# Two-layer backbone with split fp32 products: second scale block loaded into raw-token places, first shift sum written to another place, sign of the sink logits taken later

## The chip, the cores and the metric

The kernel runs on one core of one Trainium2 chip. The metric is the time of one execution in device microseconds. Three executions of the kernel before took 1580.73, 1581.42 and 1584.02 us; the median, 1581.42 us, is the time before.

## What is computed

Two layers over 256 context tokens and 1024 latent tokens of 1024 channels. Each layer norms the tokens, scales and shifts them by numbers that a conditioning vector gives (`adaln`), mixes them (layer 0: attention in windows with sink logits; layer 1: latent attention) and adds the result behind a gate. What the change touches is the start of layer 0: `adaln`, the norm, and the product with `w_in`; and the sink logits, which join the softmax much later.

```python
def rms_norm(u, g):
    y = u * lax.rsqrt(jnp.mean(u * u, axis=-1, keepdims=True) + EPS)
    return y * g

def adaln(cond, w, bias):
    m = jax.nn.silu(cond) @ w + bias
    return jnp.split(m, 3, axis=-1)          # shift, scale, gate

def reference(x, c, ctx, c_ctx, ada_w, ada_b, norm_g, final_g, ...):
    for i in range(DEPTH):                   # DEPTH = 2
        shift_x, scale_x, gate_x = adaln(c, ada_w[i], ada_b[i])
        shift_c, scale_c, gate_c = adaln(c_ctx, ada_w[i], ada_b[i])
        hx = rms_norm(x, norm_g[i]) * (1.0 + scale_x[:, None]) + shift_x[:, None]
        hc = rms_norm(ctx, norm_g[i]) * (1.0 + scale_c) + shift_c
        if i == 0:                           # softmax over [scores, sink]
            yx, yc = window_gqa(hx, hc, a_w_in[0], a_sink[0], a_w_out[0], ...)
        else:
            yx, yc = latent_attention(hx, hc, b_w_in[0], ...)
        x = x + gate_x[:, None] * yx
        ctx = ctx + gate_c * yc              # not behind the last layer
    return rms_norm(x, final_g)
```

## The kernel before

**Numbers.** Every large product is made of fp32 operands that are split in a high and a low half; `mm3` (L128 to L130) makes one product of three matmuls: high by high, low by high, high by low. The high half of the normed tokens is written by ACT (L425), the low half by DVE (L426, which needs the high half). Weight pieces are split the same way: ACT casts the high half (L123), and L124 subtracts on POOL (now and then on DVE). So PE can only start a product when ACT and then DVE, or ACT and then POOL, are done.

**The opening.** The tokens come as ten tiles of 128 (two of context, then eight latent ones), which work in five pairs `p`. `ld_x(i)` loads a tile raw (L394, tile 0 to a place of a ring, tiles 1 to 9 to nine places of a tile `raw`); `sq_x(i)` squares it on ACT (L401), makes its norm in small operations of DVE and POOL (L402, L403) and writes the normed tile on DVE (L404) to the ring `xr`, four places at 34, 38, 42 and 48 of the arena. `T0(p, q)` turns two channel blocks of a pair by PE (L414, eight or four transposes into a PSUM bank), `H0` writes the high and low halves of the turned and scaled tokens (L425, L426), and `M0` multiplies them with the first block of `w_in` (`mm3`); its sums are copied to `Vraw` (L441, L443), one place for each pair.

**The scale and shift of layer 0.** There are two blocks of 512 scale columns and two of shift columns. The weights of the first scale block come in eight pieces (`ld_first`, L743) into the four places of the ring `astage`; `half` multiplies them with the conditioning vectors on PE (L186) and spreads the sums over partitions (`cols`, L205, then L213 and L216 on DVE). The second scale block (`ada0.fetch(3, astage)`, L179) follows in the same four places as soon as PE has read the first, is multiplied by `ada0.products` (L186) and read in `cols`. The shift blocks aren't multiplied on PE: DVE weighs them row block by row block (`weigh`, L193 for the first row block and L195 for the seven others, two conditioning vectors each), into the sums `acc0[0]` and `acc0[1]`, two places of 512 floats each. `acc0[0]` stands at 48 of the arena, where the last place of the ring `xr` is, `acc0[1]` at 42; both are read by `cols(0, ...)` (L205) only after the first projections of the next part. Layer 1's and the gate's blocks are weighed later in the same way.

**Small inputs.** `load_small` loads the unit matrix, two small tables and the sink logits on ACT's DMA queue (`load2`), and L161 turns the sign of the sink logits on DVE (16 numbers in each of 128 partitions). All the large loads of the opening go through SP's queue (`load`); the program lets at most eight transfers be under way on the two queues together, and each further one waits for the eighth before it.

**What sets the order.** The code names the operations in the order above; a scheduler then moves instructions on each engine by what they wait for. The waits follow from the places: whoever writes a place waits for the last reader of what stood there.

Of the kernel before, what the change touches and what calls it, by code (L numbers as in the profile page):

```python
# [34 lines left out]
class Ring:  # L35
# [6 lines left out]
    def next(self):  # L42
        b = self.bufs[self.i % len(self.bufs)]
        self.i += 1
        return b
# [15 lines left out]
def kernel(ctx: ExitStack, tc: tile.TileContext, t, out, dbg=None):  # L61
    nc = tc.nc
# [29 lines left out]
    def f_at(kb, *dims):  # L92
        n = int(np.prod(dims))
        return shp(F[:, int(kb * KB) : int(kb * KB) + n], *dims)
# [58 lines left out]
    nsink = sm(16)  # L153

    def load_small():
        load2(out=ident, in_=t["ident"])
        nc.vector.reduce_sum(sel2, ident.rearrange("p (i c) -> p c i", i=4)[:, 0:2, :], AX.X)
        load2(out=adab, in_=t["adab_col"].rearrange("p (l j) -> p l j", l=2))
        load2(out=ng, in_=t["norm_g_col"].rearrange("p (l j) -> p l j", l=2))
        load2(out=nsink, in_=t["a_sink"].partition_broadcast(128))  # L160
        nc.vector.tensor_scalar_mul(nsink, nsink, -1.0)  # L161


    class AdaLN:
# [134 lines left out]

    hT = [r_at(0, 2, 8, 258)] + [r_at(16 * p + Z, 2, 8, 256) for p in range(1, NP)]  # L300
    wst = [80 + Z, 96 + Z]
    Vraw = [f_at(o, 2, 256) for o in (0, 2, 10, 12, 34)]
    cosa = f_at(0, SEQ)
    sina = f_at(10, SEQ)
    stg = Ring(F, [4, 6, 8], 512)
# [2 lines left out]
    junk = f_at(30, 512).bitcast(BF16)  # L308
    astage = Ring(F, [14, 18, 22, 26], 1024)
    mtmp, m2tmp = f_at(32, 512), f_at(46, 512)  # L310
    acc0 = [[f_at(o, 512), f_at(o + 2, 512)] for o in (48, 42)]
    acc1 = [f_at(30, 512), f_at(32, 512)]
    B32 = f_at(47, 8, 32)
    qst = Ring(F, [34, 48], 1024)
# [76 lines left out]
    def ld_x(i):  # L391
        if i == 0:
            xn[i] = xr.next()
        load(out=raw[:, i - 1, :] if i else xn[0], in_=src0(i))  # L394

    def sq_x(i):
        if i:
            xn[i] = xr.next()
        x = raw[:, i - 1, :] if i else xn[0]
        st = sm_ring()  # L400
        nc.scalar.activation(junk, x, AF.Square, accum_out=st[:, 0:1])  # L401
        nc.vector.tensor_scalar(st[:, 1:2], st[:, 0:1], 1.0 / D, EPS, ALU.mult, ALU.add)  # L402
        nc.gpsimd.tensor_tensor(st[:, 2:3], st[:, 1:2], mhalf, ALU.pow)  # L403
        nc.vector.tensor_scalar_mul(xn[i], x, st[:, 2:3])  # L404
# [353 lines left out]
    pieces.load()  # L758
    ld_x(2)
    ld_x(3)  # L760
    for i in range(2):
        sq_x(i)
    T0(0, 0)
# [1 line left out]
    T0(0, 1)  # L765
    pieces.cast()
    half(1)
    wsb = ada0.fetch(3, astage)
    pieces.load()
    ld_x(4)  # L770
    ld_x(5)
    pieces.load()
    for i in range(6, 10):
        ld_x(i)
    H0(0, 0)
    pieces.cast()
    H0(0, 1)
    for k in range(4):
        for j in range(2):
            M0(0, j, k, k + 1)  # L780
    sq_x(2)
    sq_x(3)
    T0(1, 0)
    T0(1, 1)
    H0(1, 0)
    H0(1, 1)
    ada0.products(wsb, bank0)
    ws0 = ada0.fetch(0, astage)
    m = copy_m(bank0)
    for k in range(4):  # L790
# [54 lines left out]
    for i, (gp, c) in enumerate([(1, 0), (1, 1), (2, 0), (2, 1)]):  # L845
        held.append((1, gp, c, proj_t(1, gp, c)))
        if i == 0:
            ada0.cols(0, 0, acc0[0], pst())
        if i == 1:
            ada0.cols(0, 1, acc0[1], pst())  # L850
            nc.scalar.copy(hT[0][:, 0, :, 256:258], ada0.B)
            nc.vector.tensor_sub(hT[0][:, 1, :, 256:258], ada0.B, hT[0][:, 0, :, 256:258].bitcast(F32))
            nc.vector.tensor_copy(B32[:, :, 0:2], ada0.B)
            vb = v_bias()
        if i == 2:
            next(vb)
        if i == 3:
            next(vb)
            load(out=cosa, in_=t["cos_a"])
            load(out=sina, in_=t["sin_a"])  # L860
            ada = ada_rest()
    for c in range(2):
        ps = proj_t(1, 0, c)
        for x in held[c::2]:
            post_t(*x)
        post_t(1, 0, c, ps)
        for _ in range(2):
            pieces.cast()
            pieces.load()
# [854 lines left out]
```

## Time and profile before

| | before |
|---|---|
| timed executions, us | 1580.73, 1581.42, 1584.02 (median 1581.42) |
| the profiled execution: its own time, us | 1577.64 |
| its span from the first to the last instruction, us | 1575.8 |
| mean granted clock of PE | 0.995 |
| busy, us: PEld, DVE, ACT, POOL | 1227.1, 992.6, 773.0, 753.9 |
| read from and written to HBM, MB | 144.90 and 46.15 |

The first row has the times that count; the profiled execution is a fourth one, 3.8 us below the median, and every duration of the trace comes from it. PEld is PE's loading of weights, which runs beside PE's products. An engine that is busy for a smaller share than PE can still hold it up at a place; where that happens is seen in the rows that show an idle time with its releaser in brackets, "[idle before <- who ended it]". In a row of the timeline stand the start in us from the start of the span, the length in us (of all instructions in the row, where it ends with a count), the engine, the line, the operation with what it writes and reads, and the idle time before it.

### The profile page before, as it was taken

To read this page: it belongs to the slowest core of one execution; us is meant where nothing else is said; L and a number is where in the kernel's file an instruction comes from. 1 tells how busy PE (TensorE), PEld (TensorE's weight loads), DVE (VectorE), ACT (ScalarE), POOL (GpSimd) and SP (SyncE) were. 2 spreads that over 40 slices of the span, in tenths; PEclk is the share of its full clock that TensorE was granted. 3 is DMA by queue.
4 is the path that set the end of the run, shared out by engine and by line. 5 is a ranking of instruction groups with operands and counts; after the bars stand their busy time and mean duration, and the time that the engine had idled before them with its cause. 6 is when DMAs were issued, how large, how long until landed. Compare 5 with 4: busy or idle time off the path is not lost.

```text
span 1575.8 us, 26871 instructions
## 1 busy us (share of the span) xinstructions
PE 1538.6 (98%) x9846; PEld 1227.1 (78%) x9846; DVE 992.6 (63%) x1757; ACT 773.0 (49%) x1492; POOL 753.9 (48%) x810
## 2 busy tenths in 40 slices
PE   6999999998999999998999999999999999999998
PEld 4888888886878888878998899666766766766687
DVE  3968996647777777768425202666566566567454
ACT  4432322368777777767313323454555555545322
POOL 1241211136574444544105140588688688689410
PEclk9999999999999999999999999999999999999999
DMA  9347775654343333336104753313233233244251
GB/s 335 94 151 213 200 196 158 196 151 114 94 131 103 85 91 94 95 121 197 40 9 143 264 158 94 97 41 97 65 98 98 74 87 92 61 138 112 69 167 67
DMA packets 148276, 192.83 MB, mean 122 GB/s; under 512 B 13984, under 2 KB 86176, under 8 KB 148144
## 3 DMA queue, kind: packets, MB, share of 16 engines
q1 hardware_dynamic: 146528, 188.94, 40.2%
q10 hardware_dynamic: 1616, 2.17, 0.5%
q8 instruction: 78, 1.28, 0.4%
q14 instruction: 54, 0.44, 0.1%
HBM read 144.90 MB, written 46.15 MB: 121 GB/s over the span
## 4 chain that ended last, share of the span: by engine, by line
PE 87%; DVE 5%; issue 2%; POOL 2%; ACT 2%; DMA 2%; SPq 0%; POOLq 0%; DVEq 0%; ACTq 0%
PE PB L128 14%; PE PB L129 14%; PE PB L130 14%; PE PB L1351 12%; PE PB L1373 9%; PE PB L623 5%; PE PB L664 5%; PE PB L1314 4%; PE PB L654 4%; DVE arena_f L195 1%; PE PB L1322 1%; PE PB L1402 1%; PE PB L683 1%; PE PB L205 1%; ACT arena_r L123 1%
## 5 line engine op out<-in xcount | busy, mean ns | idle before, releaser
L128 PE MATMUL PB<-arena_r 128*128 128x512 f32 (+3 forms) x1216 | 411.4, 340 | 5.5 <-ACT arena_r L425 2.4
L129 PE MATMUL PB<-arena_r 128*128 128x512 f32 (+3 forms) x1184 | 393.9, 333 | 3.8 <-DVE arena_r L426 2.4
L130 PE MATMUL PB<-arena_r 128*128 128x256 f32 (+3 forms) x1152 | 380.5, 331 | 0.3 <-DVE arena_r L124 0.3
L1365 POOL TENSOR_TENSOR arena_f<-arena_f 128x512 f32<-128x512 f32 x252 | 325.1, 1290 | 79.4 <-ACT arena_f L1357 62.6
L128 PEld LDWEIGHTS PB<-arena_r 128*128 128x128 f32 x1216 | 231.2, 191 | 32.4 <-ACT arena_r L425 4.9
L129 PEld LDWEIGHTS PB<-arena_r 128*128 128x128 f32 x1184 | 225.9, 191 | 24.9 <-DVE arena_r L426 4.4
L124 POOL TENSOR_TENSOR arena_r<-arena_f,arena_r 128x512 fp32r<-128x512 f32 x80 | 108.7, 1373 | 278.6 <-ACT arena_r L123 227.7
L130 PEld LDWEIGHTS PB<-arena_r 128*128 128x128 f32 x1152 | 219.9, 191 | 20.8 <-issue 1.3
L1357 ACT ACTIVATE arena_f<-PB 128x1024 f32<-128x1024 f32 x160 | 164.3, 1027 | 108.6 <-PE PB L1351 69.0
L1316 DVE TENSOR_REDUCE arena_f<-PB 128x1 f32<-128x1024 f32 x128 | 156.0, 1219 | 86.6 <-PE PB L1314 86.5
L1351 PE MATMUL PB<-arena_r 64*128 64x512 f32 (+1 forms) x1500 | 195.0, 392 | 0.3 <-ACT arena_f L1357 0.3
L1351 PEld LDWEIGHTS PB<-arena_r 64*128 64x128 f32 (+1 forms) x1500 | 136.6, 185 | 29.3 <-ACT arena_f L1357 1.8
L124 DVE TENSOR_TENSOR arena_r<-PB,arena_r 128x512 fp32r<-128x512 f32 x168 | 114.6, 689 | 61.0 <-ACT arena_r L123 60.1
L1373 PE MATMUL PB<-arena_f 128*64 128x512 f32 x640 | 144.4, 597 | 0.0
L637 ACT ACTIVATE arena_f<-arena_f,small 128x640 f32<-128x640 f32 (+2 forms) x160 | 119.5, 747 | 35.1 <-DVE small L634 32.6
L634 DVE CUSTOM_DVE_ANT_0 arena_f<-PB,arena_f,small 128x640 f32<-128x640 f32 (+2 forms) x176 | 125.1, 722 | 18.3 <-PE PB L623 11.7
L123 ACT CAST arena_r<-PB 128x512 fp32r<-128x512 f32 x176 | 101.8, 585 | 46.3 <-PE PB L654 44.2
L623 PE MATMUL PB<-arena_k,arena_r 128*128 128x256 f32 (+1 forms) x576 | 111.3, 308 | 1.6 <-DVE small L634 1.3
L1373 PEld LDWEIGHTS PB<-arena_f 128*64 128x64 f32 x640 | 43.1, 136 | 83.2 <-issue 80.0
L123 ACT CAST arena_r<-arena_f 128x512 fp32r<-128x512 f32 (+2 forms) x121 | 72.0, 605 | 68.0 <-DMA arena_f<-a_w_in 16.0
L654 PE MATMUL PB<-ident,arena_f 128*128 128x128 f32 x672 | 104.0, 274 | 0.7 <-DVE arena_r L124 0.3
L623 PEld LDWEIGHTS PB<-arena_k,arena_r 128*128 128x128 f32 x576 | 89.3, 188 | 14.0 <-DVE small L634 3.5
(211 smaller groups left out, 2530.5 us busy)
## 6 DMA issues: line engine op xcount, KB each, us to landing
arena_f<-ada_w SPq DMA_DIRECT2D x44, 512.0 KB, 4.7
arena_r<-q_d SPq DMA_DIRECT2D x80, 256.0 KB, 4.1
arena_r<-qn_d SPq DMA_DIRECT2D x64, 256.0 KB, 4.0
arena_r<-qr_d SPq DMA_DIRECT2D x172, 64.0 KB, 3.5
arena_f<-a_w_in SPq DMA_DIRECT2D x40, 256.0 KB, 3.4
g_d<-arena_f SPq DMA_DIRECT2D x32, 256.0 KB, 2.1
q_d<-arena_f SPq DMA_DIRECT2D x64, 128.0 KB, 2.5
qn_d<-arena_f SPq DMA_DIRECT2D x16, 512.0 KB, 5.4
```

What stands on the lines that cost most here:

```text
L123: nc.scalar.copy(hi, src)
L124: (lo_eng or nc.vector).tensor_sub(lo, src, hi.bitcast(F32))
L128: nc.tensor.matmul(o, ah, bh, start=first, stop=False)
L129: nc.tensor.matmul(o, al, bh, start=False, stop=False)
L130: nc.tensor.matmul(o, ah, bl, start=False, stop=last)
L623: nc.tensor.matmul(S[:, at : at + n], qT[:, s, hq, :], kT[:, g, k : k + n], start=s == 0, stop=s == 1)
L654: nc.tensor.transpose(pt[:, h, :], self.Ps[h][:, ci * 128 : ci * 128 + 128], ident)
L1316: nc.vector.reduce_max(mx[:, 32 + b : 33 + b], flat, AX.X, negate=True)
L1351: nc.tensor.matmul(S[:, t], k[r, c : c + 128], q[r], start=j == 0, stop=j == 4)
L1357: nc.scalar.activation(E, self.S, AF.Exp)
L1365: eng.tensor_add(self.acc, self.acc, E[:, t])
L1373: nc.tensor.matmul(self.pv[p : p + 64], Vq[:, cs[t], self.h % 4, :], E[:, t], start=i == 0, stop=i == 4)
```

## The change

Five things are altered, all in the opening.

1. The load of the sink logits leaves `load_small` and ACT's queue; it is issued on SP's queue next to the loads of the rotary tables, and the turning of the sign stands there too.
2. The second scale block (`ada0.fetch(3, ...)`) is loaded into `raw[5]` to `raw[8]`, the places of the raw tiles 6 to 9, right behind tiles 2 and 3, and no longer into the places of the first scale block. So these loads wait for no reader.
3. `ld_x(6)` to `ld_x(9)` move behind `ada0.products(wsb, ...)`, whose matmuls now are the last readers of those places.
4. `sq_x(2)` and `sq_x(3)` stand ahead of `H0(0, 0)` in the code.
5. `Vraw[4]` moves from 34 to 48 and `acc0[0]` from 48 to 34: the first sum of the shift now stands in the first place of the ring `xr`, in which tile 8 was the last to stand, instead of the last place, in which tile 7 was.

```diff
--- before.py
+++ after.py
@@ -157,8 +157,6 @@
         nc.vector.reduce_sum(sel2, ident.rearrange("p (i c) -> p c i", i=4)[:, 0:2, :], AX.X)
         load2(out=adab, in_=t["adab_col"].rearrange("p (l j) -> p l j", l=2))
         load2(out=ng, in_=t["norm_g_col"].rearrange("p (l j) -> p l j", l=2))
-        load2(out=nsink, in_=t["a_sink"].partition_broadcast(128))
-        nc.vector.tensor_scalar_mul(nsink, nsink, -1.0)
 
 
     class AdaLN:
@@ -299,7 +297,7 @@
 
     hT = [r_at(0, 2, 8, 258)] + [r_at(16 * p + Z, 2, 8, 256) for p in range(1, NP)]
     wst = [80 + Z, 96 + Z]
-    Vraw = [f_at(o, 2, 256) for o in (0, 2, 10, 12, 34)]
+    Vraw = [f_at(o, 2, 256) for o in (0, 2, 10, 12, 48)]
     cosa = f_at(0, SEQ)
     sina = f_at(10, SEQ)
     stg = Ring(F, [4, 6, 8], 512)
@@ -308,7 +306,7 @@
     junk = f_at(30, 512).bitcast(BF16)
     astage = Ring(F, [14, 18, 22, 26], 1024)
     mtmp, m2tmp = f_at(32, 512), f_at(46, 512)
-    acc0 = [[f_at(o, 512), f_at(o + 2, 512)] for o in (48, 42)]
+    acc0 = [[f_at(o, 512), f_at(o + 2, 512)] for o in (34, 42)]
     acc1 = [f_at(30, 512), f_at(32, 512)]
     B32 = f_at(47, 8, 32)
     qst = Ring(F, [34, 48], 1024)
@@ -758,6 +756,18 @@
     pieces.load()
     ld_x(2)
     ld_x(3)
+
+    class RawRing:
+        i = 5
+
+        def next(self):
+            self.i += 1
+            return raw[:, self.i - 1, :]
+
+    wsb = ada0.fetch(3, RawRing())
+    pieces.load()
+    ld_x(4)
+    ld_x(5)
     for i in range(2):
         sq_x(i)
     T0(0, 0)
@@ -765,26 +775,22 @@
     T0(0, 1)
     pieces.cast()
     half(1)
-    wsb = ada0.fetch(3, astage)
     pieces.load()
-    ld_x(4)
-    ld_x(5)
-    pieces.load()
-    for i in range(6, 10):
-        ld_x(i)
+    sq_x(2)
+    sq_x(3)
     H0(0, 0)
     pieces.cast()
     H0(0, 1)
     for k in range(4):
         for j in range(2):
             M0(0, j, k, k + 1)
-    sq_x(2)
-    sq_x(3)
     T0(1, 0)
     T0(1, 1)
     H0(1, 0)
     H0(1, 1)
     ada0.products(wsb, bank0)
+    for i in range(6, 10):
+        ld_x(i)
     ws0 = ada0.fetch(0, astage)
     m = copy_m(bank0)
     for k in range(4):
@@ -856,9 +862,11 @@
             next(vb)
         if i == 3:
             next(vb)
+            load(out=nsink, in_=t["a_sink"].partition_broadcast(128))
             load(out=cosa, in_=t["cos_a"])
             load(out=sina, in_=t["sin_a"])
             ada = ada_rest()
+            nc.vector.tensor_scalar_mul(nsink, nsink, -1.0)
     for c in range(2):
         ps = proj_t(1, 0, c)
         for x in held[c::2]:
```

The line numbers behind the change are smaller by two from L163 on (L426 is L424, L193 is L191, L205 is L203), and larger by six to eight behind the opening.

**SP's queue at the start.** These are the rows from the load of the raw tiles 2 and 3 on, first as before, then as now. `ada_w` are the weights of scale and shift, `a_w_in` the pieces of `w_in`, `x` the raw tiles.

```order
L394 DMA raw<-x 128x1024 x2
L179 DMA arena_f<-ada_w 128x2x512 x4
L339 DMA arena_f<-a_w_in 128x2x256
L394 DMA raw<-x 128x1024 x2
L339 DMA arena_f<-a_w_in 128x2x256
L394 DMA raw<-x 128x1024 x4
L179 DMA arena_f<-ada_w 128x2x512 x4
L339 DMA arena_f<-a_w_in 128x2x256 x7
```

```order
L392 DMA raw<-x 128x1024 x2
L177 DMA raw<-ada_w 128x2x512 x4
L337 DMA arena_f<-a_w_in 128x2x256
L392 DMA raw<-x 128x1024 x2
L337 DMA arena_f<-a_w_in 128x2x256
L392 DMA raw<-x 128x1024 x4
L177 DMA arena_f<-ada_w 128x2x512 x4
L337 DMA arena_f<-a_w_in 128x2x256 x3
L865 DMA small<-a_sink 128x16
L337 DMA arena_f<-a_w_in 128x2x256 x4
```

The second scale block (the first L179, now L177, ahead of the third `a_w_in`) keeps its row but goes to `raw`, and the load of the sink logits (L865) now is a row of its own behind the third piece that follows the first shift block (the second L177); the four raw tiles 6 to 9 keep their row too, and wait there.

**DVE at the start.** Before, then now; `small` holds the small tables and the norms.

```order
L141 COPY arena_f<-small 128x8x2
L402 TENSOR_SCALAR small<-small 128x1
L161 TENSOR_SCALAR small<-small 128x16
L402 TENSOR_SCALAR small<-small 128x1
L404 TENSOR_SCALAR arena_f<-arena_f,small 128x1024
L404 TENSOR_SCALAR arena_f<-raw,small 128x1024
```

```order
L141 COPY arena_f<-small 128x8x2
L400 TENSOR_SCALAR small<-small 128x1 x2
L402 TENSOR_SCALAR arena_f<-arena_f,small 128x1024
L402 TENSOR_SCALAR arena_f<-raw,small 128x1024
L211 TENSOR_TENSOR small<-PB,small 128x4
```

The sign (L161) is gone from between the small operations of the norm, ahead of the two normed context tiles (L404, now L402).

**DVE around the turning of the last pairs**, the piece from tile 8's normed tile (L404, now L402) on, before and then now.

```order
L404 TENSOR_SCALAR arena_f<-raw,small 128x1024
L426 SCALAR_TENSOR_TENSOR arena_r<-PB,small,arena_r 128x256 x2
L404 TENSOR_SCALAR arena_f<-raw,small 128x1024
L193 TENSOR_SCALAR arena_f<-arena_f,small 128x512
L426 SCALAR_TENSOR_TENSOR arena_r<-PB,small,arena_r 128x256
L195 SCALAR_TENSOR_TENSOR arena_f<-arena_f,small 128x512
L443 COPY arena_f<-PB 128x512
L426 SCALAR_TENSOR_TENSOR arena_r<-PB,small,arena_r 128x256 x2
L193 TENSOR_SCALAR arena_f<-arena_f,small 128x512
L426 SCALAR_TENSOR_TENSOR arena_r<-PB,small,arena_r 128x256
L195 SCALAR_TENSOR_TENSOR arena_f<-arena_f,small 128x512
L426 SCALAR_TENSOR_TENSOR arena_r<-PB,small,arena_r 128x256 x2
```

```order
L402 TENSOR_SCALAR arena_f<-raw,small 128x1024
L424 SCALAR_TENSOR_TENSOR arena_r<-PB,small,arena_r 128x256 x2
L402 TENSOR_SCALAR arena_f<-raw,small 128x1024
L424 SCALAR_TENSOR_TENSOR arena_r<-PB,small,arena_r 128x256
L441 COPY arena_f<-PB 128x512
L869 TENSOR_SCALAR small<-small 128x16
L424 SCALAR_TENSOR_TENSOR arena_r<-PB,small,arena_r 128x256 x6
L191 TENSOR_SCALAR arena_f<-arena_f,small 128x512
L424 SCALAR_TENSOR_TENSOR arena_r<-PB,small,arena_r 128x256
L193 SCALAR_TENSOR_TENSOR arena_f<-arena_f,small 128x512
L424 SCALAR_TENSOR_TENSOR arena_r<-PB,small,arena_r 128x256
L441 COPY arena_f<-PB 128x512
```

The copy of `M0`'s sums (L443, now L441) moves up, the sign (L869) stands directly behind it, six low halves (L424) follow in a row, and the first rows of the weighing (L193 and L195, now L191 and L193) move behind these. PE's order up to there is the old one; further on, the first reading of the shift sums (L205, now L203) stands a few products later, and the second twelve.

## The prediction

> **What bounds the kernel now.** I read the page first, then the stretches of the opening, then who waited for whom up to 130 us, then single instructions in order of time.
>
> ```profile
> span 1575.8 us, 26871 instructions
> PE 1538.6 (98%) x9846; PEld 1227.1 (78%) x9846; DVE 992.6 (63%) x1757; ACT 773.0 (49%) x1492; POOL 753.9 (48%) x810
> ...
> PE 87%; DVE 5%; issue 2%; POOL 2%; ACT 2%; DMA 2%; SPq 0%; POOLq 0%; DVEq 0%; ACTq 0%
> ```
>
> The two numbers behind an engine are its busy time and its share of the span. PE is busy 98% of it, and the chain that ends last is PE for 87%: time is gained only where PE idles, 1575.8 - 1538.6 = 37.2 us in all.
>
> ```profile
> 0.00:10.00 10.00, 1.80 (x9) 0.49 (x10) 2.01 (x13) 4.01 (x7) 1.35 (x6) 1.00 0.72 232
> 10.00:20.00 10.00, 8.31 (x55) 4.58 (x54) 3.26 (x8) 3.31 (x7) 2.93 (x3) 1.00 1.04 373
> ...
> 50.00:60.00 10.00, 8.41 (x66) 7.72 (x65) 9.71 (x15) 6.13 (x14) 5.86 (x6) 1.00 0.30 79
> 60.00:70.00 10.00, 9.18 (x74) 8.76 (x74) 10.00 (x19) 3.34 (x8) 0.62 (x1) 1.00 0.42 133
> 70.00:80.00 10.00, 10.00 (x64) 9.01 (x63) 9.89 (x16) 0.00 (x0) 0.00 (x0) 1.00 0.55 156
> 36.30:43.00 6.70, 5.86 (x27) 5.56 (x27) 4.36 (x10) 5.05 (x11) 0.86 (x2) 0.50 0.38 123
> ```
>
> Each row is a stretch, its length, the busy time of PE, PEld, DVE, ACT and POOL, the granted clock, the DMA share and GB/s. PE idles 8.20 us up to 10 us, 1.69 us in the next ten, 1.59 and 0.82 us between 50 and 70 us, and not at all from 70 us on. So whatever PE gains before 70 us moves all that follows, if nothing off PE is late by then.
>
> ```profile
> PE PB L186 <- DMA arena_f<-ada_w: 8.2, 2, 7.3
> SPq L179 <- PE PB L186: 7.8, 6, 2.9
> PE PB L129 <- DVE arena_r L426: 2.4, 2, 1.6
> SPq L743 <- DMA small<-a_sink: 1.3, 1, 1.3
> ```
>
> Each row: who waited, for whom, us in total, times, the longest. PE waits for scale weights twice, both in the first ten us (L743's pieces of the first scale block). The loads that the change puts elsewhere (L179, the second block) made SP's queue wait 7.8 us, but no row has PE waiting for what they bring. The other wait of PE is for DVE.
>
> **The opening: sink logits out of the first loads.**
>
> ```profile
> 2.81 6.42 DMA arena_f<-ada_w
> ...
> 9.27 1.70 PE L186 MATMUL PB<-arena_f 128*32 128x256 f32 x6 [0.86 <-DMA arena_f<-ada_w]
> 10.90 1.12 PE L414 MATMUL PB<-ident,arena_f 128*128 128x128 f32 x4
> 11.95 0.80 PE L186 MATMUL PB<-arena_f 128*32 128x256 f32 x6
> 12.68 0.66 PE L414 MATMUL PB<-ident,arena_f 128*128 128x128 f32 x4
> ...
> 9.08 0.17 DVE L161 TENSOR_SCALAR small<-small 128x16 f32<-128x16 f32 x1 [2.48 <-DMA small<-a_sink]
> 9.23 0.74 DVE L404 TENSOR_SCALAR arena_f<-arena_f,small 128x1024 f32<-128x1024 f32 x1
> 10.42 0.75 DVE L404 TENSOR_SCALAR arena_f<-raw,small 128x1024 f32<-128x1024 f32 x1 [0.45 <-POOL small L403]
> ```
>
> The first row is a link of the chain: a piece of the scale weights issued at 2.81 us lands after 6.42 us, at 9.23, and PE starts on it at 9.27 after idling 0.86 us. Meanwhile DVE stood 2.48 us on the sink logits' load (L161, until 9.08), and only then normed the two context tokens (L404, done at 9.97 and 11.17). So the four turnings at 10.90 took 1.12 us where the next four took 0.66: they waited for the second token, 0.46 us. After the change L161 is gone from DVE, its load from ACT's queue and from the first eight in flight, so SP's 1.3 us wait for it goes too, and the pieces behind are issued one place earlier. Both waits gone would give 0.86 + 0.46 = 1.3 us. The next limit is the landing of the following pieces, which no row shows: if they land as now, the products end at about 12.5 instead of 11.95 + 0.80 = 12.75, a gain of 0.3. I take **0.7 us**, between 0.3 and 1.3 and nearer the 0.86 that a row shows. From there the order on PE and ACT is the old one, so this shift is carried on.
>
> **The second block into raw's places: nothing.** Its products stand where they stood on PE and waited for no load, so an earlier load brings nothing. What it costs is that tokens 6 to 9 are loaded behind those products.
>
> ```profile
> 24.15 1.04 PE L186 MATMUL PB<-arena_f 128*32 128x512 f32 x2
> ...
> 39.37 1.05 ACT L401 ACTIVATE arena_f<-raw 128x1024 bf16<-128x1024 f32 x1
> ...
> DMA to landing us min/median/max: 4.3/7.3/10.2
> ```
>
> The first pair of products is done some 1.1 us after 24.15, that is at 25.3; token 6's load, issued then, is there at 25.3 + 7.3 = 32.6 by the median landing of such a load and at 35.5 by the longest, against the square at 39.37 that reads it. These 3.9 us of cover are the smallest; tokens 7 to 9 follow by a product each and are squared up to 47 us. If the cover were gone, every us of lateness would stop ACT, in order, and PE behind it. The sums of the second block's shift (T0, H0 and the products) keep their rows too, so moving `sq_x(2)` and `sq_x(3)` in the code costs nothing either.
>
> **The weighing behind the last turning: the main gain.** The swap of places lets the first weighing write where token 8 stood, not token 7, so it waits for token 8's turning, and DVE reaches it six L426 later.
>
> ```profile
> 52.28 4.42 POOL L124 TENSOR_TENSOR arena_r<-arena_f,arena_r 128x512 fp32r<-128x512 f32 x3 [1.36 <-ACT arena_r L123]
> ...
> 55.12 0.91 ACT L425 ACTIVATE arena_r<-PB,small 128x256 fp32r<-128x256 f32 x2 [0.97 <-PE PB L414]
> ...
> 54.04 1.50 DVE L193 TENSOR_SCALAR arena_f<-arena_f,small 128x512 f32<-128x512 f32 x1
> 55.86 1.38 DVE L195 SCALAR_TENSOR_TENSOR arena_f<-arena_f,small 128x512 f32<-128x512 f32 x1
> 57.16 0.68 DVE L443 COPY arena_f<-PB 128x512 f32<-128x512 f32 x1
> 57.77 0.86 DVE L426 SCALAR_TENSOR_TENSOR arena_r<-PB,small,arena_r 128x256 fp32r<-128x256 f32 x2
> 58.55 0.47 DVE L193 TENSOR_SCALAR arena_f<-arena_f,small 128x512 f32<-128x512 f32 x1
> 59.34 1.83 DVE L195 SCALAR_TENSOR_TENSOR arena_f<-arena_f,small 128x512 f32<-128x512 f32 x1
> ...
> 54.36 0.28 PE L130 MATMUL PB<-arena_r 128*128 128x256 f32 x1
> 58.29 0.38 PE L129 MATMUL PB<-arena_r 128*128 128x256 f32 x1 [1.58 <-DVE arena_r L426]
> 61.62 0.38 PE L129 MATMUL PB<-arena_r 128*128 128x256 f32 x1 [0.82 <-DVE arena_r L426]
> ```
>
> L193 and L195 are the weighing. Beside POOL's casts they take 1.50, 1.38 and 1.83 us, where the L193 at 58.55 took 0.47; and the low halves (L426) that PE waits for stand behind them. PE stops from 56.7 (58.29 - 1.58) until 58.29 and again before 61.62: 1.58 + 0.82 = 2.4 us. With six L426 in a row (0.43 us each by the 0.86 for two, each behind ACT's high half), the copy at 57.16 then stands ahead of them, directly behind the products that end at 54.36 + 0.28 = 54.6, and is done at 54.7 + 0.7 = 55.4. The first low half waits for its high half (55.12 + 0.46) and is ready at 56.0, and PE wants it at 56.7; the later ones follow the turnings as fast as PE makes them. So the whole **2.4 us** goes, at most 2.6 with two gaps below the listing; at least 1.4 if ACT's high halves, next in line, hold PE up for a us.
>
> **The sign of the sink logits: a new op in that row.** It stands on DVE between the copy and the six L426, at about 55.4, while POOL runs its third cast (52.28 + 4.42 = 56.7). All six L426, and PE's products of them, queue behind it. Its load is no price: it goes out behind the piece that SP issued at 38.4 us and is wanted 17 us later.
>
> ```profile
> 18.04 1.27 POOL L124 TENSOR_TENSOR arena_r<-arena_f,arena_r 128x512 fp32r<-128x512 f32 x1 [4.76 <-ACT arena_r L123]
> ...
> 18.41 0.92 DVE L216 SCALAR_TENSOR_TENSOR small<-small 128x4 f32<-128x4 f32 x1
> ```
>
> The op itself ran 0.17 us at 9.08, with POOL idle. But a 4-column op of DVE took 0.92 us at 18.41 beside a cast of POOL that ended at 18.04 + 1.27 = 19.31; and L193, an op of the new one's kind, 1.50. So it costs between 0.1 (free) and 1.3 (held from 55.4 to 56.7, with none of it in hand), and I take held: the first low half is then ready at 57.1 instead of 56.0, 0.4 behind the 56.7 at which PE wants it, and the turnings and high halves behind it make the next two pairs late by what I put at 0.2 each: **0.8 us** lost.
>
> The Trainium skill, "SBUF — State Buffer", section "Who interferes with whom", says that VectorE's single-source ops in their two-port mode and GpSimd share a port pair under an exclusive lock, the later one blocked until the earlier ends. The 0.92 and 1.50 us above agree with that; by the rule the op is held, and the sum is the one below; by the op's own 0.17 us it would be 0.7 us better.
>
> **Sum.** -0.7 - 2.4 + 0.8 = -2.3 us. The profiled execution took 1577.64 us (span 1575.8 and 1.8 around it), which would become 1575.3. The three timed runs have a median of 1581.42, 3.8 us above it; I carry the difference over: **1579.1 us**. About 0.2% (3.2 us) is what a measurement of this kernel can tell from no change.
>
> What is late next is the weighing itself.
>
> ```profile
> 74.82 9.36 DVE L195 SCALAR_TENSOR_TENSOR arena_f<-arena_f,small 128x512 f32<-128x512 f32 x14
> ...
> 77.06 1.68 PE PB L205 x16
> ...
> 86.62 1.46 PE PB L205 x14
> ```
>
> Its two sums are read by L205's products at 77.06 and from 86.62 on; the last weighing ends at 84.18 now. Without the 1.03, 0.71 and 1.16 us lost beside POOL, and with some 2.5 us of waiting for the turnings in their place, it ends at about the same time, while PE comes 2.4 us sooner but has the second reading twelve products (0.23 us each) later in its order: about 2 us are left there, and next to nothing at the first reading, which is the step most easily wrong.
>
> **Rivals.**
> - *Free sign.* The op slips between two casts, and the loads come as early as the waits allow: -1.0 - 2.4 + 0.1, **1578.1**. For it: POOL changes ops near 55.2. Chance 0.24.
> - *Loads land as before.* The sink load was not what slowed the first pieces: -0.3 - 2.4 + 0.8, **1579.5**; or nothing of the change is seen but the late wait moved to L205, 1580.5. Against it: rate and issue both dip while that load is in flight. Chance 0.18.
> - *The clock.* Between 36.3 and 43.0 us PE ran at a granted clock of 0.50, busy 5.86 us of 6.70, which cost about half of that, 2.9 us. If the shifted opening escapes it: **1576.2**, chance 0.09. If it draws a second such stretch on dense products (6.7 / 2 = 3.3 us): -2.3 + 3.3, **1582.4**, slower than before; it decides once 4.6 us of added half clock eat the gain. Against it: from 50 to 80 us the clock is 1.00 in spite of the stops. Chance 0.11.
>
> The Trainium skill, "TensorE: Matmul & The Clock Gate", Part 1, has the gate judge activity in free-running windows of about 3.4 us that do not start with the kernel. The 6.70 us stretch is close to two of them; by that rule the stretch may come or go with the phase of a run, which is the rival just named, and no run here shows more than one phase.
>
> **How the numbers follow.** The forecast has the remaining 0.38, with a range of its own from 1577.9 to 1580.3. Range for 8 in 10: from 1575.8 (clock escaped) to 1582.7 (second stretch). Faster by over 0.2% means below 1578.3: a quarter of the forecast's 0.38, two thirds of the free sign, the escaped clock, some of the rest: 0.37. Slower means above 1584.6: half of the second stretch, 0.06. Same: 0.57.
>
> **What would show it.** Opening: no DVE wait for the sink logits, the turnings at 0.66 us, PE's products done near 12.0. Weighing: no stop of PE before L129 between 54 and 62 us, first weighing after 59. Sign: its DVE row near 1 us long, or 0.1. Cover: no wait of ACT's squares for raw. Wrong would be a new PE wait before L205 (or L203 in the new numbering) near 74 us, or a half-clock stretch of another length.

## The result and the profile after

| | before | changed |
|---|---|---|
| median of 21 timed executions each, us | 1581.42 (1577.55 to 1585.44) | 1578.29 (1574.16 to 1582.69) |
| ratio to before, 95% interval | | 0.9978 (0.9969 to 0.9987) |
| profiled execution and its span, us | 1577.64, 1575.8 | 1574.73, 1573.0 |

The changed kernel is faster by 3.1 us in the medians, by 2.1 to 4.9 us by the interval, where 2.3 us were forecast. First the page of the changed kernel: span, busy times and the chain.

```profile
span 1573.0 us, 26868 instructions
PE 1538.7 (98%) x9846; PEld 1228.6 (78%) x9846; DVE 993.5 (63%) x1757; ACT 772.8 (49%) x1492; POOL 753.8 (48%) x810
...
PE 81%; DVE 8%; issue 3%; DMA 3%; ACT 2%; POOL 2%; SPq 0%; DVEq 0%; POOLq 0%; ACTq 0%
```

PE's busy time is that of before to 0.1 us; the span lost 2.8 us of idle time. The stretches of the opening and the waits, with the columns of before:

```profile
0.00:10.00 10.00, 2.64 (x12) 0.90 (x13) 2.72 (x13) 4.01 (x7) 1.76 (x6) 1.00 0.84 269
10.00:20.00 10.00, 8.29 (x53) 5.07 (x52) 2.86 (x7) 3.51 (x8) 2.53 (x2) 0.98 1.06 397
...
50.00:60.00 10.00, 9.70 (x79) 9.06 (x77) 7.46 (x13) 5.67 (x13) 5.38 (x4) 1.00 0.32 95
60.00:70.00 10.00, 10.00 (x79) 9.66 (x78) 10.00 (x19) 2.73 (x6) 0.00 (x0) 1.00 0.29 72
...
36.30:43.00 6.70, 5.74 (x38) 5.75 (x39) 4.86 (x13) 5.42 (x12) 1.04 (x2) 0.75 0.89 319
```

Who waited for whom, us in total, times, the longest:

```profile
PE PB L184 <- DMA arena_f<-ada_w: 7.4, 1, 7.4
PE PB L129 <- DVE arena_r L424: 0.4, 2, 0.3
SPq L392 <- PE PB L184: 11.6, 3, 8.8
```

PE is 0.84 us busier in the first ten us and 1.29 and 0.82 us between 50 and 70 us. Its second stop for scale weights is gone (one wait in place of two), and 0.4 us are left of the 2.4 us before L129. SP's queue now waits 11.6 us with the raw tiles 6 to 9, and nothing waits for that. Single instructions of PE:

```profile
7.36 2.39 PE L184 MATMUL PB<-arena_f 128*32 128x256 f32 x10 [7.36 <-DMA arena_f<-ada_w]
9.68 1.12 PE L412 MATMUL PB<-ident,arena_f 128*128 128x128 f32 x4
10.73 1.07 PE L184 MATMUL PB<-arena_f 128*32 128x256 f32 x6
11.74 1.12 PE L412 MATMUL PB<-ident,arena_f 128*128 128x128 f32 x4
12.65 0.61 PE L203 MATMUL PB<-small,arena_f 128*128 128x2 f32 x4
...
53.25 1.04 PE L412 MATMUL PB<-ident,arena_f 128*128 128x128 f32 x8
55.74 0.38 PE L129 MATMUL PB<-arena_r 128*128 128x256 f32 x1 [0.27 <-DVE arena_r L424]
61.46 1.04 PE L412 MATMUL PB<-ident,arena_f 128*128 128x128 f32 x8
...
95.62 1.03 PE L459 MATMUL PB<-arena_f,small 128*128 128x256 f32 x4
```

POOL and DVE around the turnings:

```profile
51.03 4.24 POOL L124 TENSOR_TENSOR arena_r<-arena_f,arena_r 128x512 fp32r<-128x512 f32 x3 [1.52 <-ACT arena_r L123]
...
54.05 1.25 DVE L869 TENSOR_SCALAR small<-small 128x16 f32<-128x16 f32 x1
55.22 0.86 DVE L424 SCALAR_TENSOR_TENSOR arena_r<-PB,small,arena_r 128x256 fp32r<-128x256 f32 x2
...
60.30 0.48 DVE L191 TENSOR_SCALAR arena_f<-arena_f,small 128x512 f32<-128x512 f32 x1
```

The ten first scale products run without a stop from 7.36 us, and `cols` (L203) starts at 12.65, where it started at 13.24. The sign (L869) took 1.25 us beside POOL's third cast, against 0.17 at 9.08 before, and the first low half behind it made PE stop for 0.27 us before 55.74. The weighing (L191) begins at 60.30, behind six low halves. Three marks of PE, which the experiments use too, tell where the time went:

```profile
54.48 1.04 PE L414 MATMUL PB<-ident,arena_f 128*128 128x128 f32 x8
...
65.03 1.03 PE L414 MATMUL PB<-ident,arena_f 128*128 128x128 f32 x8
...
98.98 1.02 PE L461 MATMUL PB<-arena_f,small 128*128 128x256 f32 x4
```

(1) The first `cols`, L205 or L203: 13.24 before, 12.65 now, 0.59 us won. (2) From there to the eight turnings with which the last stretch of turnings begins: 54.48 - 13.24 = 41.24 and 53.25 - 12.65 = 40.60, 0.64 won, in which the half clock differs. (3) From these to the last eight turnings: 65.03 - 54.48 = 10.55 and 61.46 - 53.25 = 8.21, 2.34 won. (4) From there to L461 (L459): 98.98 - 65.03 = 33.95 and 95.62 - 61.46 = 34.16, 0.21 lost.

This last figure is work that changed its place and no time lost: one product of 512 columns, 0.23 us, stands ahead of the last eight turnings in the kernel before and behind them in the changed one (its row comes with the weighing, below), so (3) and (4) are best read together: 44.50 - 42.37 = 2.13 won. At L459 the four marks make 3.36 us; the span is shorter by 2.8 us, so 0.6 of it are lost again later. Where isn't shown; PE's busy time is smaller by 0.3 us from 200 to 300 us (99.32 against 99.62) and by 0.4 from 700 to 800 us (94.46 against 94.87), but these stretches don't hold quite the same work before and after.

### The profile page after: what moved, and what is told of

It reads as the page before. It is cut to its first block, busy times and chain, and to the rows that moved or that the text cites. A ratio compares the mean times of both kernels' runs of the same rounds, so it can differ in the third digit from the quotient of the medians.

```text
span 1573.0 us, 26868 instructions
## 1 busy us (share of the span) xinstructions
PE 1538.7 (98%) x9846; PEld 1228.6 (78%) x9846; DVE 993.5 (63%) x1757; ACT 772.8 (49%) x1492; POOL 753.8 (48%) x810
## 4 chain that ended last, share of the span: by engine, by line
PE 81%; DVE 8%; issue 3%; DMA 3%; ACT 2%; POOL 2%; SPq 0%; DVEq 0%; POOLq 0%; ACTq 0%
PE PB L128 12%; PE PB L129 12%; PE PB L130 12%; PE PB L1359 12%; PE PB L1381 9%; PE PB L621 5%; PE PB L662 5%; PE PB L1322 4%; PE PB L652 4%; DVE arena_f L193 2%; DVE arena_f L519 1%; DMA arena_f<-a_w_in 1%; PE PB L1330 1%; PE PB L1410 1%; ACT arena_r L123 1%
## 5 line engine op out<-in xcount | busy, mean ns | idle before, releaser
L128 PE MATMUL PB<-arena_r 128*128 128x512 f32 (+3 forms) x1216 | 410.8, 339 | 5.5 <-ACT arena_r L423 2.4
L129 PE MATMUL PB<-arena_r 128*128 128x512 f32 (+3 forms) x1184 | 395.2, 334 | 1.8 <-POOL arena_r L689 0.8
L128 PEld LDWEIGHTS PB<-arena_r 128*128 128x128 f32 x1216 | 231.1, 191 | 32.2 <-ACT arena_r L423 4.8
L129 PEld LDWEIGHTS PB<-arena_r 128*128 128x128 f32 x1184 | 226.4, 191 | 22.9 <-DVE arena_r L424 2.4
L632 DVE CUSTOM_DVE_ANT_0 arena_f<-PB,arena_f,small 128x640 f32<-128x640 f32 (+2 forms) x176 | 125.2, 722 | 19.5 <-PE PB L621 11.6
```

The costliest lines, as they stand in the source:

```text
L128: nc.tensor.matmul(o, ah, bh, start=first, stop=False)
L129: nc.tensor.matmul(o, al, bh, start=False, stop=False)
```

## The experiments

All ratios are to the kernel before on the same chip. A distance between two marks of PE tells tenths of a us, if the same work stands between them, where a median of a dozen executions that spread over 5 to 9 us tells one or two.

### One part at a time

**The sink part alone.** The kernel before with this edit:

```diff
-        load2(out=nsink, in_=t["a_sink"].partition_broadcast(128))
-        nc.vector.tensor_scalar_mul(nsink, nsink, -1.0)
...
+            load(out=nsink, in_=t["a_sink"].partition_broadcast(128))
             load(out=cosa, in_=t["cos_a"])
             load(out=sina, in_=t["sin_a"])
             ada = ada_rest()
+            nc.vector.tensor_scalar_mul(nsink, nsink, -1.0)
```

> The kernel before with the sink part alone (load on SP's queue, sign later; the sign then stands far back on DVE, among the weighing rows). Theory (the sink logits' load and sign hold up the start): PE starts its second run of scale products without a stop, the first product of hidden tokens (the first L128) starts 0.6 us earlier than 14.86, at about 14.3, the two stops before L129 (1.58 and 0.82) stay, and the last eight turnings (65.03 before, 61.46 in the changed kernel) start at 64.4, or at 63.8 if the half clock moves to the place that it has in the changed kernel. Time 0.6 to 1.2 us below before. Rival (the start gains by the earlier loads of the second block): the first L128 stays at 14.8 to 14.9 and the time is that of before.

1579.66 us, ratio 0.9993 (0.9982 to 1.0004), which by itself isn't told from no change; the marks are. Its `cols` started at 12.74, half a us earlier than before, and the last turnings at 64.72, 0.31 earlier; the two stops before L129 stayed (10.55 us for the stretch). Here the scheduler put the sign among the later weighings:

```profile
83.88 0.16 DVE L861 TENSOR_SCALAR small<-small 128x16 f32<-128x16 f32 x1
...
92.88 4.18 POOL L124 TENSOR_TENSOR arena_r<-arena_f,arena_r 128x512 fp32r<-128x512 f32 x3 [32.59 <-PE PB L450]
```

With POOL idle until 92.88 the sign took 0.16 us. The gain of the opening belongs to the sink part; the rival, that the earlier second block brings it, falls (and see the second block alone, below).

**The swap of places alone.** The kernel before with

```diff
-    Vraw = [f_at(o, 2, 256) for o in (0, 2, 10, 12, 34)]
+    Vraw = [f_at(o, 2, 256) for o in (0, 2, 10, 12, 48)]
...
-    acc0 = [[f_at(o, 512), f_at(o + 2, 512)] for o in (48, 42)]
+    acc0 = [[f_at(o, 512), f_at(o + 2, 512)] for o in (34, 42)]
```

> The kernel before with the swap of places alone (Vraw[4] and acc0[0]). Theory: the opening is that of before (first L128 at 14.86), the two stops of 2.4 us before L129 are gone, the last eight turnings start at 62.6, and the reading of the first shift sum stays within 0.5 us of waiting: time 2.0 to 2.4 us below before. Rival (the wait only moves): the turnings start at 62.6 too, but PE waits some 2 us before the reading of the shift sums near 75 us, and the time is that of before.

1577.92 us, ratio 0.9982 (0.9970 to 0.9994). The stretch of the turnings took 62.30 - 54.89 = 7.41 us:

```profile
54.89 1.04 PE L414 MATMUL PB<-ident,arena_f 128*128 128x128 f32 x8
...
62.30 0.93 PE L414 MATMUL PB<-ident,arena_f 128*128 128x128 f32 x7
```

The same stretch by windows, of this kernel and of the one before:

```profile
54.89:62.30 7.41, 7.39 (x63) 7.16 (x62) 4.66 (x11) 3.90 (x9) 3.30 (x3) 1.00 0.49 142
```

```profile
54.48:65.03 10.55, 8.14 (x65) 7.45 (x63) 10.55 (x17) 3.90 (x9) 3.50 (x3) 1.00 0.53 149
```

PE is busy 7.39 of these 7.41 us, and was busy 8.14 of 10.55 before. The stretch is 3.14 us shorter, but not all of this is time won. PE's order is not quite the old one here: the turnings between the two marks now go in pieces of 1, 2, 1 and 4 instead of 4, 2 and 2, and the product of 512 columns that started at 59.38 before comes behind the last eight turnings. Up to L461, where both kernels have done the same work, it took 98.98 - 54.48 = 44.50 us before and 96.47 - 54.89 = 41.58 us here. So the swap is worth 2.92 us, still more than the 2.4 us of listed stops, and PE did not wait at the reading of the shift sums: the rival falls. The first reading is now cut in two (2 and 14 rows), as the second was before already; with the four products beside it it took 2.73 us before and 2.70 in the changed kernel, so the cut costs nothing.

**The second block alone.** The changed kernel with the sink part and the swap undone:

```diff
     ld_x(3)
+    class RawRing:
...
+    wsb = ada0.fetch(3, RawRing())
...
-    wsb = ada0.fetch(3, astage)
...
     ada0.products(wsb, bank0)
+    for i in range(6, 10):
+        ld_x(i)
```

> The kernel before with the second scale block in raw's places and the raw tiles 6 to 9 loaded behind its products, alone. Theory: no instruction of PE waits for these loads before or after, so the first L128 stays at 14.8 to 14.9, the last eight turnings at 64.9 to 65.2, and the time within 0.3 us of before. Rival 1 (the block brings the gain of the opening): first L128 at 14.3. Rival 2 (the raw tiles come late): ACT's squares (L399 or L401) wait for raw near 38 us, and the turnings start after 65.5.

1581.29 us, ratio 1.0004 (0.9993 to 1.0016): nothing that can be told. `cols` came at 13.43, and the distances behind it are those of before to 0.01 us: 41.25 to the eight turnings, 10.55 for the turnings' stretch. ACT's squares did not wait for the raw tiles 6 to 9.

**Everything but the sink part.**

```diff
+        load2(out=nsink, in_=t["a_sink"].partition_broadcast(128))
+        nc.vector.tensor_scalar_mul(nsink, nsink, -1.0)
...
-            load(out=nsink, in_=t["a_sink"].partition_broadcast(128))
...
-            nc.vector.tensor_scalar_mul(nsink, nsink, -1.0)
```

> The changed kernel with the sink part undone (load on ACT's queue and sign in the first small operations, as before); the second block and the swap of places stay. Theory: the opening is the old one (first L128 at 14.8 to 15.1), the last stretch of turnings runs at full pace, 7.4 us from the eight turnings of the last pair but one to those of the last pair (10.55 before, 8.21 in the changed kernel, 7.40 with the sign on ACT), so that the eight last turnings start at 62.0 to 62.6. The part's two effects, 0.6 us won at the start and 0.8 lost at the turnings, nearly cancel, and the time is within 0.5 us of that of the changed kernel. Rival (the sink part is a gain on the whole): 0.6 us or more above the changed kernel.

1579.06 us, ratio 0.9978 (0.9963 to 0.9992), that of the changed kernel, as expected. The turnings' stretch was 62.48 - 55.09 = 7.39 us. The opening came out later than expected, `cols` only at 14.36; the last section gives the likely reason.

### The price of the sign

**The sign on ACT**, in the changed kernel:

```diff
-            nc.vector.tensor_scalar_mul(nsink, nsink, -1.0)
+            nc.scalar.activation(nsink, nsink, AF.Copy, scale=-1.0)
```

> The changed kernel with the sign of the sink logits taken by ACT in place of DVE, at a place where ACT stood idle. Theory (the sign is held on DVE by POOL's cast, 1.25 us instead of 0.17, and pushes the low halves behind it): the stops before L129 (0.27 and those below the listing) go, the last eight turnings start 0.3 to 0.8 us earlier, at 60.7 to 61.2 instead of 61.46, and the time is 0.3 to 0.8 us below that of the changed kernel. Rival (the high halves of ACT and PE's own work set the pace there): the turnings stay at 61.3 to 61.5.

1577.13 us, ratio 0.9975 (0.9964 to 0.9985). ACT took 0.21 us for it while it waited for PE anyway:

```profile
52.61 0.21 ACT L869 ACTIVATE small<-small 128x16 f32<-128x16 f32 x1
...
53.04 1.04 PE L412 MATMUL PB<-ident,arena_f 128*128 128x128 f32 x8
...
60.44 1.04 PE L412 MATMUL PB<-ident,arena_f 128*128 128x128 f32 x8
```

The stretch is 60.44 - 53.04 = 7.40 us, against 8.21 with the sign on DVE: its price is 0.81 us. It is neither the operation itself (0.16 us with POOL idle) nor its load, only its place beside POOL's cast.

Both again, timed side by side:

> The changed kernel with the sign on ACT, once more, beside the changed kernel on the same chip. Theory: first L128 at 14.2, last stretch of turnings 7.4 us, time 0.8 us below that of the changed kernel (the intervals of both will overlap). Rival: no difference in time.

> The changed kernel, for the comparison with the one above: 3 us below before, ratio 0.998; last stretch of turnings 8.2 us, first L128 at 14.2 to 14.3.

1577.08 us, ratio 0.9965 (0.9952 to 0.9978), and 1577.38 us, 0.9967 (0.9956 to 0.9978). The stretches were 60.60 - 53.19 = 7.41 and again 8.2 us, but the times cannot be told apart: the version with the sign on ACT beats the other in the trace, by 0.8 us, and not in a measurement of this size. Against before the changed kernel won 4.5 us here, more than the 3 expected, and its first L128 came earlier than expected, at 13.77.

### The load or the wait?

Before, the sink logits could hold the start in two ways: their load took one of the eight places of SP's and ACT's queues, and DVE waited for it. This kernel is the changed one with the load early and the sign late:

```diff
+    late = sm(1)
...
         load2(out=ng, in_=t["norm_g_col"].rearrange("p (l j) -> p l j", l=2))
+        load2(out=nsink, in_=t["a_sink"].partition_broadcast(128))
...
-            load(out=nsink, in_=t["a_sink"].partition_broadcast(128))
...
-            nc.vector.tensor_scalar_mul(nsink, nsink, -1.0)
+            nc.vector.tensor_scalar(late, acc0[1][0][:, 0:1], 0.0, -1.0, ALU.mult, ALU.add)
+            nc.vector.tensor_scalar_mul(nsink, nsink, late)
```

> The changed kernel with the sink logits' load back on ACT's queue, among the first eight, but with the sign left far back on DVE, behind the weighing (its factor is made from a sum that is ready only there; one operation of one column more). It parts the two ways in which the sink logits can hold up the start. Theory A (the load takes one of the eight places and delays the pieces): PE stops again before its second run of scale products, by 0.4 to 1.0 us, and the first L128 starts at 14.6 to 15.2. Theory B (DVE's wait for the load is what counts): the first L128 starts at 14.2 to 14.3 as in the changed kernel. With both: half of the way. In any case the sign takes 0.17 us and the last stretch of turnings 7.4 us.

1579.93 us, ratio 0.9986 (0.9973 to 0.9998), on the chip where the changed kernel had 0.9967. The marks account for only a part of these 2.5 us: L461 began 0.64 us later than in the changed kernel's profile there (96.48 against 95.84); the rest stays open. The stretch of the turnings took 7.41 us, as expected.

```profile
7.83 0.75 DVE L404 TENSOR_SCALAR arena_f<-arena_f,small 128x1024 f32<-128x1024 f32 x1
9.03 0.75 DVE L404 TENSOR_SCALAR arena_f<-raw,small 128x1024 f32<-128x1024 f32 x1 [0.45 <-POOL small L403]
...
9.48 1.69 PE L186 MATMUL PB<-arena_f 128*32 128x256 f32 x6 [1.06 <-DMA arena_f<-ada_w]
...
13.15 1.12 PE L414 MATMUL PB<-ident,arena_f 128*128 128x128 f32 x4
14.06 0.74 PE L205 MATMUL PB<-small,arena_f 128*128 128x2 f32 x4
```

And SP's queue there:

```profile
SPq L743 <- DMA small<-a_sink: 1.5, 1, 1.5
```

DVE normed the two context tokens as early as in the changed kernel (7.83 and 9.03, against 7.82 and 9.01 in its timed repeat), and still PE stopped 1.06 us for weights, SP 1.5 us for the place that the sink's load held, and `cols` began at 14.06, the first L128 at 15.82, later even than theory A had it (the last section gives the likely reason). It is the load's place in the queue that counts. DVE's wait shows no price of its own: 14.06 lies among the five profiles that have both the early load and the wait (13.24 to 14.36).

### The clock

The second mark's 0.64 us were not forecast. The changed kernel and the one before were profiled again:

> The changed kernel once more, for the place of its half-clock stretches. Theory (windows of 3.4 us that don't follow PE's work: a window in which PE idled much is followed by one at half clock): stretches of 3.4 us or twice that, beginning within 0.5 us of 19.6 and 36.5; the second one ends at 40 if it began late enough to hold less of the idle time before the turnings near 37.2, else at 43. Rival (the stretch is set by the work, as it stands): 36.8 to 40.2 again, to 0.1 us. The stretch of the last turnings stays at 8.2 us in any case.

> The changed kernel a third time: as for the second. If the stretch at 36.5 ends at 40 in all three, the 0.6 us that it saves belong to the change; if it ends at 43 in one, they are drawn from run to run.

> The kernel before once more, for its half-clock stretches. Theory: one stretch of 6.8 us beginning at 36.2 to 36.9, none near 20 us; the stretch of the last turnings 10.5 us. Rival (the place is drawn anew in each run): a stretch of 3.4 us, or one near 20 us.

In the rows that follow stand the stretch, its length, the busy time of PE, PEld, DVE, ACT and POOL, the granted clock, the DMA share and GB/s. The changed kernel, first profile:

```profile
36.76:40.17 3.41, 2.91 (x14) 2.92 (x15) 2.70 (x8) 2.85 (x7) 0.55 (x1) 0.50 0.99 361
40.17:43.59 3.42, 3.42 (x31) 3.42 (x31) 2.20 (x7) 2.59 (x7) 1.08 (x2) 1.00 0.63 217
```

Its second profile:

```profile
35.96:39.37 3.41, 2.31 (x12) 2.12 (x11) 3.04 (x7) 2.85 (x6) 0.61 (x2) 0.50 1.04 393
39.37:42.79 3.42, 3.42 (x18) 3.42 (x17) 1.70 (x5) 2.06 (x6) 0.00 (x0) 0.50 0.83 289
```

The kernel before, second profile:

```profile
37.18:40.59 3.41, 2.28 (x20) 2.26 (x20) 3.13 (x7) 3.32 (x8) 0.55 (x1) 1.00 0.54 169
57.66:61.07 3.41, 3.41 (x17) 3.31 (x16) 3.41 (x5) 1.49 (x4) 1.27 (x1) 0.50 0.20 40
```

From 36 us on the changed kernel had one stretch of 3.41 us in its first profile and two in a row in the second and the third, and in the first and the third one more near 20 us; the kernel before had two in a row in its first profile and none there in the second, but one from 57.66 us. So the expectation for before failed (its stretch of turnings, with half clock from 57.66, took 11.04 us), the changed kernel's second profile lacked the stretch near 20 us that was expected, and the rival holds: the stretches are drawn from run to run. From the first `cols` to the eight turnings it was 39.30 us with none (53.06 - 13.76), 40.4 to 40.8 with one near 37 us, 41.2 to 41.4 with two, in both kernels alike (41.24 before, 54.03 - 12.69 = 41.34 for the changed kernel). The other three profiles of the changed kernel have 41.3 to 41.4, as the first one of before. So the 0.64 us of the first pair of profiles are such a draw and no part of the change.

## Why the prediction was right

**The bound.** PE's idle time before 70 us is what moved, and PE's order behind it carried it on, as forecast.

**The opening, 0.7 us forecast.** 0.59 us in the first pair of profiles. Over all profiles `cols` began at 13.24 to 14.36 us with the sink's load among the first (six profiles, mean 13.74) and at 12.15 to 12.83 without (seven, mean 12.63): 1.1 us, or 0.9 without the two profiles in which PE's slow start lasted one stretch longer (14.06 and 14.36; see the last section). So the size was near and rather too small, the cause (the load among the first) was right, and one step behind the size was wrong: the 1.12 us of four turnings at 10.90, read as a wait of 0.46 us for the second token. In the changed kernel four turnings took 1.12 us at 9.68 and again at 11.74, when both tokens had been there since 9.87 (9.12 + 0.75). PE ran at half its pace until 12.35 us before and 12.87 us in the changed kernel (both worked out in the last section), and the granted clock, 1.00 in these rows, doesn't show it.

**The second block, nothing forecast.** Nothing: 1.0004, the same distances between the marks, and no wait of ACT's squares for the raw tiles 6 to 9.

**The weighing, 2.4 us forecast, the term that was mis-sized.** The swap alone is worth 2.92 us up to L461. The forecast added up the two listed stops, 1.58 and 0.82. But PE's products right behind a stop run longer and further apart. In the kernel before, L129 at 58.29 took 0.38 us instead of 0.28, and the next ones came 0.22 and 0.29 us later instead of 0.12:

```profile
58.51 0.28 PE L130 MATMUL PB<-arena_r 128*128 128x256 f32 x1
58.80 0.39 PE L128 MATMUL PB<-arena_r 128*128 128x256 f32 x1
59.02 0.60 PE L414 MATMUL PB<-ident,arena_f 128*128 128x128 f32 x4
59.38 0.48 PE L128 MATMUL PB<-arena_r 128*128 128x512 f32 x1
```

From 58.29 to the turnings at 59.02 three products took 0.73 us, where three take 0.36 without a stop: 0.37 more. And a listed stop is counted from the end of the instruction before it, while without a stop the next one starts 0.12 us behind that one's start: the product before the first stop lasted 0.28 us, the two turnings before the second 0.38, so the stops cost 0.16 and 0.25 more than listed. Of these 0.8 us the swap kernel loses some 0.3 itself, behind a turning at 57.31; the other 0.5 are the difference between 2.4 and 2.9. None of it stands in a row of waits. The upper end that was given, 2.6, was too low. (The last row is the wide product that now comes later.)

**The sign, 0.8 us lost.** Measured 0.81 (8.21 - 7.40), by the mechanism that was named: held to the end of POOL's cast at 51.03 + 4.24 = 55.27, it ended at 54.05 + 1.25 = 55.30; in the three other profiles of the changed kernel it took 1.25 us again, ending 0.03 to 0.04 us behind the cast. That the size fits so well is partly luck: the forecast had the first low half late by 0.4 us and put 0.2 us each for the next two pairs. The first L129 did come 0.42 us later behind the eight turnings than with the sign on ACT (55.74 - 53.25 = 2.49 against 55.11 - 53.04 = 2.07), but the other 0.4 us were lost right behind that stop (behind the next turning, 56.77 - 53.25 = 3.52 against 55.75 - 53.04 = 2.71), and nothing at the later pairs. The Trainium skill, "SBUF — State Buffer", section "Who interferes with whom", has VectorE's operations with a single input in their two-port mode locked out while GpSimd holds the shared ports. The trace agrees: 0.16 us with POOL idle, 1.25 beside its cast. Of the two rows that the prediction set beside this, the 1.50 us fit it; the 0.92 us are of an operation with two inputs (L216), of which the passage as given there doesn't speak.

**What is late next.** The step called most easily wrong held: PE did not wait for the weighing at either reading. The last weighing ended at 84.13 us (84.18 before) and the second reading began at 85.35, so 1.2 us were left where about 2 were forecast; that reading stands fourteen products later than before, not twelve. The fourteen rows of the first reading began at 74.69, 0.6 us behind the end of its weighing (74.06).

**The sum.** -0.59 - 2.92 + 0.81 = -2.7 us from the first pair's marks, or -3.2 with the mean of the opening (12.63 - 13.74 = -1.1), beside 3.1 measured: the opening was forecast too small by up to 0.4 and the weighing by 0.5, the others are right to 0.1. The number alone would have misled: 1578.29 lies nearer to the 1578.1 of the free sign than to the forecast, and the sign was not free.

**The signs.** No wait of DVE for the sink logits, the first weighing behind 59 us (60.30), a sign of about 1 us (1.25) and no wait of ACT's squares came as said. The turnings at 0.66 us did not (1.12), and one stop before L129, the 0.27 us that the sign makes, remained. The half-clock stretch had another length, 3.41 us, which the prediction named as a sign of being wrong; the repeats show it to be a draw.

**The rivals.** The free sign falls (1.25 us). Loads that land as before fall for the opening, and a wait moved to L205 falls too. The rivals on the clock were real in kind, but the stretches come and go between profiles of one kernel. A second stretch, near 20 us, came in two of the four profiles of the changed kernel and in neither of the kernel before, which is too few to say whether the change makes it likelier. It cost next to nothing where it came (41.44 us to the eight turnings with it, 41.34 and 41.32 without, each with two near 37 us), since PE, slowed there, no longer waited for the norm of the tiles 2 and 3 (the 0.9 us before L414 of the kernel before).

## What to carry to other kernels

The price of a stop of PE is the distance between two of its instructions between which the same work stands before and after, not the listed wait; here 2.9 us against 2.4. A scheduler can move work across a mark, and then the distance lies: here by 0.2 us, from 2.9 to 3.1. A tiny operation on DVE costs what stands behind it on that engine: with a cast of POOL beside it, a sign of 16 columns cost 0.8 us, and on an engine that waits at that place nothing. Of the first transfers of a kernel each one counts, however small, when their number is limited: 8 KB held the weights back by a us.

## What the runs showed of the hardware

PE starts slow, and where that ends is drawn with the same clock as the later stretches. In all thirteen profiles the half-clock stretches begin and end on one raster of 3.41 us, whose place against the span's start differs from run to run. On that raster an edge fell at 12.35 us before (36.24 - 7 x 3.413), at 12.87 in the changed kernel's first profile (36.76 - 7 x 3.413), at 11.45 in the changed kernel's timed repeat, and at 11.14 and 14.55 in the kernel with the early load. First the repeat, the window up to the edge:

```profile
8.04:11.45 3.41, 3.41 (x18) 1.28 (x16) 1.28 (x2) 0.62 (x1) 1.76 (x2) 1.00 1.09 383
```

Its PE rows on both sides of that edge:

```profile
9.61 1.12 PE L412 MATMUL PB<-ident,arena_f 128*128 128x128 f32 x4
10.66 1.00 PE L184 MATMUL PB<-arena_f 128*32 128x256 f32 x6
11.59 0.66 PE L412 MATMUL PB<-ident,arena_f 128*128 128x128 f32 x4
```

The kernel with the early load, up to 11.14 us and behind it:

```profile
7.72:11.14 3.42, 2.35 (x11) 0.41 (x7) 1.60 (x3) 0.00 (x0) 1.02 (x1) 1.00 0.95 301
11.14:14.55 3.41, 3.41 (x18) 2.27 (x18) 0.00 (x0) 0.99 (x2) 1.27 (x1) 1.00 1.04 364
```

In the changed kernel's repeat PE was busy all of the stretch up to 11.45, and its turnings went from 1.12 us for four to 0.66 at 11.59. In the kernel with the early load PE was busy 2.35 of the 3.42 us up to 11.14, because of its stop for weights, and stayed slow until 14.55 (turnings of 1.12 us still at 13.15); the kernel with everything but the sink part, with 2.62 us up to 11.34, until 14.75. In the eleven other profiles PE was busy 3.07 us or more of the stretch up to the edge where it became fast. So a stop in the opening can cost another 3.41 us of half pace: which would be why the early load costs 0.6 us in one run and above a us in another; it was not tried by itself. The Trainium skill, "TensorE: Matmul & The Clock Gate", Part 1, has PE throttled until it has been busy for about 3.4 us in free-running windows; the raster agrees with it. What share of a window must be busy stays open: 3.07 us of 3.41 were enough to end the slow start of the kernel before; in the first profile of the kernel before the half clock followed a stretch in which PE was busy 2.34 us, and in its repeat none followed one with 2.28 us (the row at 37.18 above). The first of these two cases, by windows:

```profile
32.83:36.24 3.41, 2.34 (x17) 1.69 (x16) 1.36 (x5) 2.33 (x6) 0.64 (x2) 1.00 1.05 407
36.24:39.65 3.41, 2.57 (x11) 2.27 (x12) 2.73 (x7) 2.85 (x7) 0.92 (x2) 0.50 0.51 166
```

PE idled 1.07 us of the 3.41 in the first row, and the clock is 0.50 in the second.
